# Row sums of a 64 MB array on one Trainium2 core: the wait for the last store stands on TensorE in place of SyncE

## The chip, the core and the metric

One NeuronCore of a Trainium2 chip runs the program. Its engines take part as follows: VectorE (DVE in the profile) and ScalarE (ACT) add, GpSimd (POOL) and SyncE (SP) issue transfers, and TensorE (PE) has no work. The metric is the device time of one execution in microseconds; lower is better. Each engine has a sequencer that runs its instructions in order; a wait is an instruction of its own there, and everything behind it on that engine stays back until the semaphore has the value that is asked for.

## What is computed

```python
def setup_inputs():
    batch, seq, dim = 32, 512, 1024
    return {"x": np.random.randn(batch, seq, dim).astype(np.float32)}

def reference(x: np.ndarray) -> np.ndarray:
    return np.sum(x, axis=-1).astype(np.float32)
```

16,384 rows of 1024 float32 numbers (67.1 MB) are read, and one sum for each row (65.5 KB) is written.

## The kernel before

The rows are split over the 128 partitions, so each partition has 128 rows to sum. They are loaded in blocks of 16 rows per partition (8 MB) into three buffers in turn. SyncE issues the first load alone, a half block of 8 rows per partition (L100), which a function at the end of the build (L9 to L27) moves ahead of everything else in SyncE's program. GpSimd issues all others (L102): seven whole blocks, and the last eight rows per partition in four pieces. From the third block on it waits (L156) until VectorE has summed the block whose buffer is filled again.

VectorE sums the half block and six whole blocks with one reduction each (L109). The last whole block and the last eight rows are cut small, to leave little work after the last byte: VectorE adds the halves of a row and accumulates (L118), and ScalarE copies rows into PSUM, where nobody reads them, with an accumulated sum (L138), nine rows in all. All sums stand in one tile, `sums`.

Three stores write the sums. ScalarE issues two of them after its last activation has been started (L215, L216) and then waits until both have landed (L217). SyncE issues the third: it waits for VectorE's last sum (L230) and ScalarE's last sum (L231), stores the last 16 columns of `sums` (L232, 8 KB), and waits until that store has landed (L233). That is the last instruction of the program. The build merges the wait of L230 into the store itself.

TensorE has a few instructions in all: its part in the barriers at the start of the program, recorded under L248 and L43 (the records of its sequencer carry the name PEldq), and one branch (L259) into the block that holds the kernel. In the kernel itself it has none.

After the program come instructions that are not in the kernel's file: the engines meet, the semaphores are set to zero, and the engines meet once more. The profile's span ends with the program's own last instruction, so this end lies outside of the span. It is not in any view of the page; the trace keeps the times at which semaphores were changed there.

Of the kernel before, what the change touches and what calls it, by code (L numbers as in the profile page):

```python
# [30 lines left out]
def kernel(  # L31
# [5 lines left out]
    nc = tc.nc  # L37
# [53 lines left out]
    def semaphore(name):  # L91
        return ctx.enter_context(nc.semaphore(name=name))
# [136 lines left out]
    stored = semaphore("stored")  # L229
    nc.sync.wait_ge(done, 1)  # L230
    nc.sync.wait_ge(acts, n_acts)  # L231
    nc.sync.dma_start(out=out_b[:, TWO - BIG :], in_=sums[:, J - BIG :]).then_inc(stored, 16)  # L232
    nc.sync.wait_ge(stored, 16)  # L233


# [28 lines left out]
```

## Time and profile before

| what | value |
|---|---|
| median of 3 runs | 160.44 us (160.31 to 160.48) |
| the profiled execution | 160.33 us |
| its span, first to last instruction of the program | 159.0 us |
| HBM traffic over the span | 67.11 MB read, 0.07 MB written, 422 GB/s |
| busy: VectorE, ScalarE, GpSimd | 121.6, 10.9, 6.1 us |
| the last store, issue to landing | 1.4 us |

Times in views count from the start of the span. A trailing q in an engine's name (SPq, ACTq, PEldq) means its sequencer: waits, branches and DMA issues, which do not count as busy. TensorE does not appear among the busy engines. The trace's list of semaphore changes gives a time for each change; where several engines change the same semaphore in turn, the engine is told by the order and by what it did just before.

### The profile page before, as it was taken

To read this page: it belongs to the slowest core of one execution; us is meant where nothing else is said; L and a number is where in the kernel's file an instruction comes from. 1 tells how busy PE (TensorE), PEld (TensorE's weight loads), DVE (VectorE), ACT (ScalarE), POOL (GpSimd) and SP (SyncE) were. 2 spreads that over 40 slices of the span, in tenths; PEclk is the share of its full clock that TensorE was granted. 3 is DMA by queue.
4 is the path that set the end of the run, shared out by engine and by line. 5 is a ranking of instruction groups with operands and counts; after the bars stand their busy time and mean duration, and the time that the engine had idled before them with its cause. 6 is when DMAs were issued, how large, how long until landed. Compare 5 with 4: busy or idle time off the path is not lost.

```text
span 159.0 us, 124 instructions
## 1 busy us (share of the span) xinstructions
DVE 121.6 (76%) x43; ACT 10.9 (7%) x19; POOL 6.1 (4%) x15
## 2 busy tenths in 40 slices
DVE  0000009999998999949999599986999679995986
ACT  3000000000000000000000000000000000000995
POOL 3000000010001000010000100000000220000000
DMA  7999996997969969969969979799699699698994
GB/s 264 527 396 396 396 659 264 528 462 330 527 280 511 527 264 527 527 264 527 527 264 527 478 313 527 346 445 528 264 527 527 264 528 527 264 527 349 402 407 177
DMA packets 2000, 67.18 MB, mean 422 GB/s; under 512 B 624, under 2 KB 624, under 8 KB 848
## 3 DMA queue, kind: packets, MB, share of 16 engines
q0 software_dynamic: 1424, 62.92, 91.4%
q1 hardware_dynamic: 288, 4.20, 6.6%
q10 hardware_dynamic: 288, 0.06, 0.2%
HBM read 67.11 MB, written 0.07 MB: 422 GB/s over the span
## 4 chain that ended last, share of the span: by engine, by line
DMA 73%; DVE 24%; issue 1%; POOL 0%; POOLq 0%
DMA rows<-in_x_dram 73%; DVE sums L109 22%; DVE rows L118 2%; POOL rows L102 0%; DVE ends L118 0%; DVE sums L118 0%; POOLq L43 0%
## 5 line engine op out<-in xcount | busy, mean ns | idle before, releaser
L109 DVE TENSOR_REDUCE sums<-rows 128x16 f32<-128x16384 f32 (+1 forms) x7 | 111.9, 16000 | 31.8 <-DMA rows<-in_x_dram 31.8
L138 ACT ACTIVATE unread<-rows 128x1024 f32<-128x1024 f32 x9 | 9.1, 1014 | 145.1 <-DMA rows<-in_x_dram 145.1
L118 DVE CUSTOM_DVE_ANT_0 rows<-rows 128x512 f32<-128x512 f32 (+2 forms) x15 | 8.9, 663 | 2.6 <-DMA rows<-in_x_dram 2.6
L102 POOL DMA_DIRECT2D rows<-in_x_dram x9 | 4.9, 544 | 122.0 <-DVE sums L109 120.5
L138 ACT ACTIVATION_READ_ACCUMULATOR unread<-rows 128x1 f32 x9 | 1.7, 187 | 0.0
L138 ACT ACT_TABLE_LOAD x1 | 1.3, 1283 | 1.4 <-PEq L43 1.4
L118 DVE DVE_READ_ACCUMULATOR2_ANT sums<- 128x1 f32 x15 | 1.3, 84 | 0.0
L175 DVE MEMSET ends<- 128x1 f32 x2 | 0.1, 59 | 1.5 <-PEq L43 1.5
L102 POOL DMA_DIRECT2D ends<-in_x_dram x2 | 1.1, 541 | 0.0
L118 DVE CUSTOM_DVE_ANT_0 ends<-ends 128x257 f32<-128x257 f32 (+1 forms) x2 | 0.6, 360 | 0.0
L118 DVE DVE_READ_ACCUMULATOR2_ANT ends<- 128x1 f32 x2 | 0.2, 84 | 0.0
L248 POOL MEMSET const-float32-0.0<- 128x1 f32 x1 | 0.1, 98 | 0.2 <-issue 0.2
L248 POOL MEMSET const-bfloat16-1.0<- 128x1 bf16 x1 | 0.1, 101 | 0.0
L248 POOL MEMSET const-float32-1.0<- 128x1 f32 x1 | 0.1, 98 | 0.0
L248 POOL MEMSET const-uint8-127<- 128x1 uint8 x1 | 0.1, 98 | 0.0
## 6 DMA issues: line engine op xcount, KB each, us to landing
rows<-in_x_dram SPq DMA_DIRECT2D x1, 4096.0 KB, 24.1
rows<-in_x_dram POOLq DMA_DIRECT2D x1, 2816.0 KB, 27.8
rows<-in_x_dram POOLq DMA_DIRECT2D x1, 896.0 KB, 29.5
ends<-in_x_dram POOLq DMA_DIRECT2D x1, 256.0 KB, 29.6
ends<-in_x_dram POOLq DMA_DIRECT2D x1, 128.0 KB, 29.3
rows<-in_x_dram POOLq DMA_DIRECT2D x7, 40.4
out_dram<-sums ACTq DMA_DIRECT2D x1, 48.0 KB, 1.6
out_dram<-sums ACTq DMA_DIRECT2D x1, 8.0 KB, 1.5
```

The costliest lines, as they stand in the source:

```text
L102: nc.gpsimd.dma_start(out=dst, in_=src, single_packet=True).then_inc(sem, 16)
L109: return nc.vector.tensor_reduce(out=sums[:, j : j + n], in_=block, axis=mybir.AxisListType.X, op=mybir.AluOpType.add,)
L118: return nc.vector.tensor_tensor_reduce(out=src[:, :n], in0=src[:, :n], in1=src[:, n:], scale=1.0, scalar=0.0, op0=mybir.AluOpType.add, op ...
L138: nc.scalar.activation(out=unread[n_acts % len(unread)][:, :], in_=src, func=mybir.ActivationFunctionType.Copy, accum_out=sums[:, j : j + ...
L175: nc.vector.memset(w[:, -1:], 0.0)
L248: nc = _bacc.Bacc("TRN2", target_bir_lowering=False, num_devices=1)
```

## The change

```diff
     nc.sync.wait_ge(done, 1)
     nc.sync.wait_ge(acts, n_acts)
     nc.sync.dma_start(out=out_b[:, TWO - BIG :], in_=sums[:, J - BIG :]).then_inc(stored, 16)
-    nc.sync.wait_ge(stored, 16)
+    nc.tensor.wait_ge(stored, 16)
```

The wait for the last store is taken from SyncE and given to TensorE. SyncE's program then ends with the issue of the store. On TensorE the wait comes right behind the branch into the kernel's block, so its sequencer arrives there at the start and stays until the store has landed. All other instructions and their order on each engine are unchanged.

## The prediction

> **What bounds the kernel now.** I first read the page's chain of work that ended last.
>
> ```profile
> DMA 73%; DVE 24%; issue 1%; POOL 0%; POOLq 0%
> DMA rows<-in_x_dram 73%; DVE sums L109 22%; DVE rows L118 2%; POOL rows L102 0%; DVE ends L118 0%; DVE sums L118 0%; POOLq L43 0%
> ```
>
> The loads and VectorE's sums behind them fill it. The change touches none of them: TensorE issues no load and holds no buffer. So the span up to the last store is taken as it is, and the question is what follows. The timeline's last lines (start, length, instruction) and SyncE's waits come next.
>
> ```profile
> 157.47 0.09 DVE L118 DVE_READ_ACCUMULATOR2_ANT sums<- 128x1 f32 x1
> 157.59 0.35 SPq L232 DMA_DIRECT2D out_dram<-sums  x1
> ```
>
> ```profile
> SPq L231 <- ACT unread L138: 156.1, 1, 156.1
> SPq L233 <- DMA out_dram<-sums: 1.1, 1, 1.1
> ```
>
> VectorE's last sum releases the store at 157.59 us; SyncE then sits 1.1 us in the wait that is to be moved. The views of the single waits L233 and L217 (ScalarE's, for the two earlier stores) give their places:
>
> ```profile
> L233 SPq EVENT_SEMAPHORE  x1: 17/17/17, 159.0 to 159.0; - x1
> ```
>
> ```profile
> L217 ACTq EVENT_SEMAPHORE  x1: 17/17/17, 158.3 to 158.3; - x1
> ```
>
> L233 is the last instruction; the span ends 17 ns after its start. But the execution took 160.33 us and the span 159.0, so 1.3 us lie around it, and that is where this change works. There I read the trace's list of semaphore changes. To the nanosecond, the last of the 16 steps of the store's semaphore is at 158.995 and L233 is recorded from 159.012. Of semaphore 2, which the program does not name, the list has:
>
> ```
>   1.644
> 158.431  158.469  158.513
> 159.153  159.197  159.235  159.269  159.318
> (runs of other semaphores, each changed once: 159.278 to 159.880)
> 160.104  160.138  160.177  160.221  160.244  160.343  160.381  160.415  160.462
> ```
>
> I read these as two rounds of nine, each passed along the five engines and back, with a stretch of resets between. In the first round, one engine hands on at 1.644, and only TensorE has nothing to do from then on. The next step comes at 158.431, 131 ns after ScalarE's L217; two more follow by 38 and 44 ns; then all wait for SyncE, which hands on at 159.153, 141 ns after L233. The way back takes 44, 38, 34 and 49 ns, to TensorE at 159.318. So TensorE is first in the row and SyncE last, and the late engine of today is the one with only the way back ahead of it: 159.318 - 159.153 = 165 ns. The Trainium skill bears this reading out: its page "Runtime: NRT & Kernel Launch", under "Semaphores 0–2 are reserved", calls number 2 the sync barrier.
>
> What follows hangs on TensorE too. The longest run of resets, semaphores 7 to 53, begins at 159.533, 215 ns after that last step, and ends at 159.880, when the other four runs are over by 159.681. The second round starts 224 ns later. So whatever delays 159.318 delays the end by as much.
>
> **The change, part by part.** *Taken away:* SyncE's wait. SyncE can hand on about 1.1 us earlier (its store's issue ends at 157.59 + 0.35 = 157.94 us), but it still has to be reached through TensorE, so this gains nothing by itself. Nothing stands behind L233 on SyncE and no DMA is moved; no queue is passed.
>
> *Added:* a wait on TensorE, which stands there from 1.4 us on. Queued behind it is no instruction of the program, only the hand-on that today comes at 1.644; for that, all four other engines wait in the first round. What it costs is worked out in three terms.
>
> First, how soon TensorE sees the semaphore. The barriers at the start release all engines; their records carry L43 (and L248).
>
> ```profile
> L43 SPq EVENT_SEMAPHORE  x2: 17/17/17, 1.0 to 1.3; - x2
> L43 ACTq EVENT_SEMAPHORE  x2: 17/17/17, 1.0 to 1.4; - x2
> L43 PEldq EVENT_SEMAPHORE  x2: 51/51/51, 1.0 to 1.4; - x2
> ```
>
> TensorE's such instruction takes 51 ns where SyncE's takes 17, and in these records it begins 12 ns after SyncE's (1.359 against 1.347, 1.031 against 1.019). I take 12 ns, with 0 as the lower bound since part of it may be the order of the release.
>
> Second, from that wait to the hand-on. SyncE's row is 141 ns. TensorE's only row is 1.359 to 1.644 = 285 ns. It has the branch of L259 in it, which the changed end has not. On ScalarE the same wait and branch lead to the next start in 77 ns (1.351 to 1.428), and without a branch, ahead of a drain, in 92 (0.696 to 0.788): the branch shows no price there. TensorE is slow without a branch as well: 150 ns from wait to drain (0.704 to 0.854). I therefore take 285 ns, as the one row of the engine and step in question, so 285 - 141 = +144 ns. The lower bound is ScalarE's row of 131 ns at the end, which would give -10; scaling that row by TensorE's slowness, 131 x 150 / 92 = 214, gives +73. By the Trainium skill, page "Advanced Engine Details and Errata", section "Control Flow Timing", an unconditional branch takes about 51 ns; taking that off as an estimate leaves 234 ns, and the sum below would be +0.30 us.
>
> Third, the way that is left. With TensorE late, the first engine is late, and the round goes out and back after it. The last round shows a whole one with nobody late: 160.104 to 160.462 = 358 ns (34, 39, 44, 23 out, then 99, 38, 34, 47 back). The round just ahead of the program takes 373 (-0.375 to -0.002). In place of 165 that is +193 ns, or +208 by the longer one.
>
> The sum: 12 + 144 + 193 = +349 ns, with the bounds 0 - 10 + 193 = +183 below and 12 + 144 + 208 = +364 above. Long parking of TensorE needs no further term: ahead of the program it handed on at -7.531, sat until the way back of that round, and made its step 50 ns behind its neighbour, as the 49 and 47 above. The two calm rounds and the resets stay as long as they are.
>
> The profiled execution at 160.33 us would thus become 160.68. It lies 0.11 under the median of the runs; on the median of 160.44 the forecast is **160.79 us**, 0.22% slower. Its span should grow only by 12 + (51 - 17) = 46 ns, to 159.1, as the rest lies behind it.
>
> **The rivals.** *TensorE's hand-on is cheaper than its one row.* For it speaks the branch in that row, and the scaled 214 ns; against it, that no TensorE row shows the cheaper price. The sum with 214 is 12 + 73 + 193 = +278 ns, with ScalarE's own price +183: 160.62 to 160.72. From 256 ns downward the sum stays under 0.32 us, which is 0.2%.
>
> *A round costs the same whoever is late.* Then only the first two terms count, 12 + 144 = +156 ns: 160.60. The 358 ns of the last round speak for a fixed price, the 165 ns behind SyncE's step speak against it. The Trainium skill gives the rule in "Runtime: NRT & Kernel Launch", section "The ~15µs preamble/postamble breakdown": about 355 ns for eight hops between the five engines. Its length agrees with the 358 measured; that it is paid whole after the last arrival does not agree with the 165.
>
> *The wait holds nothing back: faster.* If the step at 1.644 is not TensorE's, or TensorE takes its part in the round without having passed the wait, nobody waits for the store any more. SyncE would then answer 23 ns after the step at 158.513 (as in the last round), at 158.536 in place of 159.153: 0.617 us less, so 159.82, and faster as soon as over 0.32 us of it remain. For it: the result lands anyway before the end at 160.46. Against it: an engine runs in order, and SyncE and ScalarE both handed on only after their waits.
>
> *A dearer wake.* TensorE might need longer after 157 us in a wait than after 1; the 5 us at the launch showed no such price. If its own 285 ns came twice, the sum is 349 + 285 = +634 ns: 161.07.
>
> **How the numbers follow.** A measurement of this kernel can tell about 0.2%, 0.32 us, from no change. I give the forecast, with TensorE's price near its own row and a full round, 0.57; the cheaper hand-on 0.24; the round with a fixed price 0.06; the wait that holds nothing 0.07; the dearer wake 0.06. Slower is the forecast and the dearer wake, 0.63; same is the cheaper hand-on and the fixed round, 0.30; faster 0.07. The range has the bounds of the sum, 160.62 to 160.80, and the fixed round at 160.60; runs of the same kernel spread from 0.13 under to 0.04 over their median, so about 0.1 us is added below and 0.13 above: 160.50 to 160.93. The faster rival and the dearer wake stay outside.
>
> **What would show it.** In the profile after, L233 must be a record of TensorE's sequencer, 51 ns long, beginning about 30 ns after the store's last step, and the span about 159.1. The early step of semaphore 2 must be gone; its first step after the store must come about 0.3 us behind the last landing, and nine steps must follow one another within some 0.36 us, with no gap for SyncE. If the first step comes 0.2 us behind the landing, the second term was too large; if fewer than nine steps follow it, the order of the engines is not the one I read. A step of the round ahead of the landing, or a time under 160.1, would prove the forecast wrong altogether; so would a store that is issued or lands later, since I hold everything before it unchanged.

## The result, and the profile after

| | before | after |
|---|---|---|
| median of 22 runs each | 160.31 us (160.23 to 160.66) | 160.68 us (160.55 to 161.37) |
| ratio, 95% interval | | 1.0023, 1.0017 to 1.0029 |
| the profiled execution | 160.33 us | 160.59 us |
| its span | 159.0 us | 159.0 us |

The change makes the kernel slower by 0.23%, some 0.37 us. The span is 159.0 us in both profiled executions, so the loss is to be looked for behind it. First the page of the changed kernel: the opening, the busy engines, and the chain that ended last.

```profile
span 159.0 us, 124 instructions
DVE 121.6 (77%) x43; ACT 10.9 (7%) x19; POOL 6.2 (4%) x15
DMA 74%; DVE 22%; POOL 1%; issue 1%; POOLq 0%
```

The busy times are those of before to 0.1 us, and the transfers have 74% of the chain where they had 73% (it ends through another of the last loads, so VectorE has 22% in place of 24%). That is the same kernel up to the last store. The timeline's last lines, the view of line 233, and SyncE's waits show the end of the program:

```profile
157.37 0.08 DVE L118 DVE_READ_ACCUMULATOR2_ANT sums<- 128x1 f32 x1
157.48 0.35 SPq L232 DMA_DIRECT2D out_dram<-sums  x1
```

```profile
L233 PEldq EVENT_SEMAPHORE  x1: 51/51/51, 158.9 to 158.9; - x1
```

```profile
SPq L231 <- ACT unread L138: 156.0, 1, 156.0
SPq L43 <- PEq L43: 0.5, 2, 0.3
SPq L248 <- PEq L248: 0.2, 1, 0.2
```

The record of L233 has gone to TensorE's sequencer and takes 51 ns in place of 17, and SyncE's wait of 1.1 us for the store is no longer listed. The store is issued 0.11 us earlier than in the execution shown of before, which is where the two executions differ inside the span.

The rest is in the trace's list of semaphore changes. Here are the steps of semaphore 2 in nanoseconds from the last landing of the last store (158.995 us before, 158.894 us after), with the early step of the calm start where there is one:

```
before  early at 1.644 us; ScalarE, GpSimd, VectorE by -564, -526, -482
        158  202  240  274  323
        1109 1143 1182 1226 1249 1348 1386 1420 1467
after   no early step
        319  353  391  435  459  556  596  630  677
        1465 1500 1538 1581 1605 1703 1741 1775 1822
```

The early step is gone: it was TensorE's. All nine steps of the first round now come behind the landing, and they take 677 - 319 = 358 ns, as the calm last round does (358 ns before, 357 after). From the last step of the first round to the last of the second it is 1144 ns before and 1145 after. So the end grew by 1822 - 1467 = 355 ns. In the profiled executions the store landed 101 ns earlier after the change, and 355 - 101 = 254 ns is the 0.26 us between their times. In all eleven profiled executions of this document, the measured time is 0.12 to 0.14 us less than the time of that last step counted from the span's start: the measured time moves with the last step of semaphore 2.

### The profile page after: what moved, and what is told of

Read it like the earlier page. It is cut to its first block, busy times and chain, and to the rows that moved or that the text cites. A ratio compares the mean times of both kernels' runs of the same rounds, so it can differ in the third digit from the quotient of the medians.

```text
span 159.0 us, 124 instructions
## 1 busy us (share of the span) xinstructions
DVE 121.6 (77%) x43; ACT 10.9 (7%) x19; POOL 6.2 (4%) x15
## 4 chain that ended last, share of the span: by engine, by line
DMA 74%; DVE 22%; POOL 1%; issue 1%; POOLq 0%
DMA rows<-in_x_dram 56%; DVE sums L109 22%; DMA ends<-in_x_dram 19%; POOL rows L102 1%; DVE ends L118 0%; DVE sums L118 0%; POOLq L43 0%
```

## The experiments

All but one are edits of the kernel before, at L233; the one that doubles TensorE's wait is an edit of the changed kernel. Each is judged by two numbers: the nanoseconds from the last landing of the last store to the last step of semaphore 2 in its profile, "the tail" from here on (1467 before, 1822 after), and the ratio of its time to that of the kernel before.

**Whose place costs what.** The wait was given to each of the other three engines.

```diff
-    nc.sync.wait_ge(stored, 16)
+    nc.scalar.wait_ge(stored, 16)
```

> Position theory (a late engine pays its own step and all of the round that is left behind it): ScalarE is second in the row, 34 ns behind TensorE, so 358 - 34 = 324 ns of the round are left after its step. Landing of the store to its wait 21 ns, wait to step 131 ns (L217's row), 324 ns, then the 1.145 us to the last step: 1.62 us from the last landing to the last step of semaphore 2, against 1.467 before and 1.822 with TensorE; the time about 0.15 us over before. Rival (TensorE costs more only because its sequencer is slow): ScalarE's own step is no slower than SyncE's, so 1.47 us and no change.

```diff
-    nc.sync.wait_ge(stored, 16)
+    nc.vector.wait_ge(stored, 16)
```

> Position theory: VectorE is read as fourth in the row, 117 ns behind TensorE, so 358 - 117 = 241 ns are left after its step. Its own step is estimated from its waits at the start, 131 x 111 / 92 = 158 ns, after 28 ns to the wait: 28 + 158 + 241 + 1145 = 1.57 us from landing to the last step, about 0.10 us over before. If VectorE is third and GpSimd fourth, 285 ns are left and it is 1.62 us. Rival (own slowness alone): 1.467 + 0.011 + 0.017 = 1.50 us.

```diff
-    nc.sync.wait_ge(stored, 16)
+    nc.gpsimd.wait_ge(stored, 16)
```

> Position theory: GpSimd is read as third, 73 ns behind TensorE, so 285 ns are left after its step. Its own step has no row at the end; between ScalarE's 131 and TensorE's 290 ns it gives 1.58 to 1.74 us from landing to the last step, 0.11 to 0.27 us over before. Rival (own slowness alone): 1.46 to 1.62 us. The place that the steps show is the main thing asked for: two steps (TensorE, ScalarE) must stand before the gap, and the late one is the third.

The views of line 233 in the three kernels, ScalarE first, then VectorE, then GpSimd:

```profile
L233 ACTq EVENT_SEMAPHORE  x1: 38/38/38, 159.0 to 159.0; - x1
```

```profile
L233 DVEq EVENT_SEMAPHORE  x1: 21/21/21, 158.9 to 158.9; - x1
```

```profile
L233 POOLq EVENT_SEMAPHORE  x1: 17/17/17, 159.0 to 159.0; - x1
```

ScalarE's record is longer than its 17 of before, because the build put the waits of L217 and of the last store into one instruction; behind the single wait of L217 in the kernel before, ScalarE's step came after 131 ns. What the semaphore changes show, with the begin of the wait's record, the engine's step, and the round's last step all counted from the landing:

| engine that waits | its wait | its step | own price (step less wait) | round's end | way left | tail | ratio to before, 95% |
|---|---|---|---|---|---|---|---|
| SyncE (before) | 17 | 158 | 141 | 323 | 165 | 1467 | |
| TensorE (after) | 29 | 319 | 290 | 677 | 358 | 1822 | 1.0023 (1.0017 to 1.0029) |
| ScalarE | 21 | 173 | 152 | 496 | 323 | 1641 | 1.0015 (1.0006 to 1.0024) |
| GpSimd | 24 | 573 | 549 | 859 | 286 | 2004 | 1.0032 (1.0019 to 1.0044) |
| VectorE | 27 | 195 | 168 | 437 | 242 | 1584 | 1.0015 (1.0006 to 1.0024) |

The way left falls from 358 through 323, 286 and 242 to 165 in the order TensorE, ScalarE, GpSimd, VectorE, SyncE. With VectorE late, two steps besides TensorE's early one stand ahead of the gap; with GpSimd late one, with ScalarE none. This settles the row that had been read from one trace. ScalarE separates the theories best: its own price is only 11 ns over SyncE's, yet its tail is 174 ns longer, and 323 - 165 = 158 of those are the way left. Slowness alone asked for no change on ScalarE. VectorE's tail came to 1584 where 1570 were expected; its ratio says that it is slower than before, but is too coarse to tell it from ScalarE. GpSimd's place was the expected one, but its own price missed the bounds, and its tail with it: 549 ns, where 131 to 290 had been given.

**Is it the wait that SyncE lost?** SyncE keeps its wait, and TensorE has one as well.

```diff
+    nc.tensor.wait_ge(stored, 16)
     nc.sync.wait_ge(stored, 16)
```

> TensorE and SyncE both wait for the store. Position theory: SyncE's wait ends 17 ns after the landing and its turn comes only some 460 ns later, so it is covered: 1.82 us from landing to the last step, as with TensorE alone, and a time 0.35 us over before. Rival (the loss comes from taking the wait off SyncE, which then reaches its end in another state): 1.47 us and no change from before.

```profile
L233 PEldq EVENT_SEMAPHORE  x1: 51/51/51, 159.0 to 159.0; - x1
```

```profile
L234 SPq EVENT_SEMAPHORE  x1: 17/17/17, 158.9 to 158.9; - x1
```

These are the views of the two waits in that kernel. The record of SyncE's begins 16 ns behind the landing, its turn in the round came at 459 ns, as after the change; the tail is 1823 ns and the ratio 1.0022 (1.0012 to 1.0031). SyncE's wait is fully covered once TensorE's is there, and taking it away gained nothing.

**Is any wait on TensorE dear?** TensorE waits for ScalarE's two stores, which land earlier, and SyncE for the last one.

```diff
+    nc.tensor.wait_ge(early, 32)
     nc.sync.wait_ge(stored, 16)
```

> SyncE waits for the last store as before; TensorE waits for the two stores of ScalarE, which landed at 158.28 us in the profile before. Position theory: TensorE's step comes about 29 + 290 = 320 ns after that landing, near 158.60, and ScalarE, GpSimd and VectorE follow by 158.72, still ahead of SyncE's step at 159.15: 1.467 us from the last landing to the last step, no change. Rival (any long wait on TensorE is dear, by a wake of its sequencer or by its late hand-on): about 0.35 us over before.

```profile
L233 PEldq EVENT_SEMAPHORE  x1: 51/51/51, 158.5 to 158.5; - x1
```

```profile
L234 SPq EVENT_SEMAPHORE  x1: 17/17/17, 159.1 to 159.1; - x1
```

Again the two waits, TensorE's first. ScalarE's stores landed at 158.441 us; TensorE's wait is 660 ns ahead of the last landing and its step 370 ns ahead: 290 ns, the same price, but now under the store's flight. ScalarE, GpSimd and VectorE follow by -254, SyncE's step comes at 157, and the tail is 1465 ns with a ratio of 0.9997 (0.9987 to 1.0008). The same wait of 157 us and the same slow hand-on cost nothing where TensorE is not the last to arrive.

**What the 290 ns are made of.** First the wait was written twice.

```diff
     nc.tensor.wait_ge(stored, 16)
+    nc.tensor.wait_ge(stored, 16)
```

> The changed kernel with the wait for the store written twice on TensorE. If TensorE's 290 ns from wait to step are its ordinary price for each instruction at the end, the second wait adds one more instruction's worth, 50 to 150 ns (51 ns is the record's length, 150 the time from such a wait to the next instruction in the start's rows): 1.87 to 1.97 us from landing to the last step, 0.40 to 0.50 us over before. Rival (the 290 ns are a wake after the long wait, paid once): 1.82 to 1.85 us.

This told nothing about the price: the build put both waits into one instruction, so the program had nothing more to do than the changed kernel. Its tail of 1817 ns and its ratio of 1.0020 (1.0007 to 1.0032) repeat that kernel. Then waits for semaphores that already had their value were set around the wait for the store; the build makes of the three one wait for the store and one further instruction behind it, which holds the other two waits. This was done on TensorE, as the edit shows, and in the same way on GpSimd and on SyncE.

```diff
-    nc.sync.wait_ge(stored, 16)
+    nc.tensor.wait_ge(early, 32)
+    nc.tensor.wait_ge(stored, 16)
+    nc.tensor.wait_ge(done, 1)
```

> TensorE waits for the store and then has one more instruction, a wait for semaphores that have long had their value. Theory: the 290 ns from TensorE's wait to its step are made of ordinary instructions of a slow sequencer, so one more adds 50 to 150 ns (the record's 51, or the 150 from such a wait to the next instruction at the start): 1.87 to 1.97 us from the last landing to the last step of semaphore 2. Rival (a wake that is paid once, the rest is cheap as on SyncE, 17 to 40 ns): 1.84 to 1.86 us.

> The same on GpSimd, whose 549 ns from wait to step were above the bounds given for it. Theory: the 549 hold a fixed piece of GpSimd's end and its plain instructions are cheap (in the start's rows two such waits stand 78 ns apart, 1.227 to 1.305 us), so one more adds 20 to 80 ns to 2.004 us: 2.02 to 2.08 us. Rival: each GpSimd instruction is dear, 150 ns and more: 2.15 us or more.

> The same on SyncE, in the kernel before. One more instruction costs 20 to 70 ns there (17 is the record's length, 71 the time from such a wait to the next instruction at the start): 1.49 to 1.54 us from landing to the last step, against 1.467. Rival (the end is bound by something other than SyncE's step): 1.467 us.

The views of the two records on TensorE, on GpSimd and on SyncE:

```profile
L234 PEldq EVENT_SEMAPHORE  x1: 51/51/51, 158.9 to 158.9; - x1
```

```profile
L235 PEldq EVENT_SEMAPHORE  x1: 51/51/51, 159.0 to 159.0; - x1
```

```profile
L234 POOLq EVENT_SEMAPHORE  x1: 17/17/17, 158.9 to 158.9; - x1
```

```profile
L235 POOLq EVENT_SEMAPHORE  x1: 43/43/43, 159.0 to 159.0; - x1
```

```profile
L234 SPq EVENT_SEMAPHORE  x1: 17/17/17, 158.9 to 158.9; - x1
```

```profile
L235 SPq EVENT_SEMAPHORE  x1: 28/28/28, 159.0 to 159.0; - x1
```

| one more instruction on | step after the landing, without and with it | begin of its record, and from there to the step | tail, without and with it | ratio to before, 95% |
|---|---|---|---|---|
| TensorE | 319, 424 | 139, 285 | 1822, 1924 | 1.0023 (1.0014 to 1.0032) |
| GpSimd | 573, 659 | 90, 569 | 2004, 2091 | 1.0036 (1.0024 to 1.0049) |
| SyncE | 158, 223 | 75, 148 | 1467, 1530 | 1.0006 (0.9995 to 1.0017) |

One trivial instruction moves the step by 105 ns on TensorE, 86 on GpSimd and 65 on SyncE. The further instruction had nothing left to wait for, and yet from its record to the step it takes as long as from the single wait for the store: 285 ns against 290 on TensorE, 148 against 141 on SyncE, 569 against 549 on GpSimd (on the last two its record is 11 and 26 ns longer than the single wait's). So these prices are not those of a wake. TensorE's 290 ns are the worth of 290 / 105 = 2.8 such instructions, SyncE's 141 of 2.2; that would fit a few ordinary steps of a slower sequencer, but no trace shows what stands between the last wait and the step. GpSimd's 549 are 6.4 of them, so something else is likely to be in them; what it is stays open. GpSimd's tail went 11 ns over the range expected. The trace resolves these steps; the times of the last kernels, with intervals of about 0.2% and more in width, do not.

No placement beat the kernel before: SyncE has the shortest way left, and of the five prices in the table the lowest hand-on (ScalarE's 131 ns behind a single wait is 10 ns less, against 158 ns more of the way). A kernel with no wait for the last store was not tried, since its end would race with the store.

## Why the prediction was right

*The stage.* The span was said to grow by 46 ns only, and the cost to lie behind it. The span stayed at 159.0 us in the profiled execution, whose store came 0.11 us earlier; from the landing to the end of the record of L233, 17 + 17 = 34 ns became 29 + 51 = 80, which is the 46.

*The three terms.* They were 12, 144 and 193 ns and measured 29 - 17 = 12, 290 - 141 = 149, and 358 - 165 = 193. The sum of 349 measured 354, and 355 with a nanosecond in the resets. In time, 0.35 us on 160.44 was forecast, and 160.68 - 160.31 = 0.37 us came. The predicted 160.79 is 0.11 over the measured median because the three runs shown of before lay 0.13 over the later median of 22.

*The choice that mattered* was TensorE's price: its own start row of 285 ns, or something cheaper. The row held, at 290 ns without a branch. That the two agree to 5 ns does not show the branch to be free, as the prediction argued from ScalarE: the end may have something in its place that costs as much, and no run separates the two, so the closeness may be luck. The Trainium skill's figure of about 51 ns for a branch ("Advanced Engine Details and Errata", "Control Flow Timing") would have led to 234 ns and +0.30 us, and the measured step decides against taking it off here.

*The rivals.* The cheaper hand-on fell with those 290 ns. A round of fixed price fell with the way left, which changes with the engine from 358 to 165 ns; the about 355 ns that the Trainium skill gives for the round ahead of a program ("Runtime: NRT & Kernel Launch", "The ~15µs preamble/postamble breakdown") agree with the way left when TensorE is the late one, 358 here, and not with the 165 to 323 of the others. The wait that holds nothing fell with the early step that is gone and the first step 319 ns behind the landing. The dearer wake, which asked for TensorE's 285 ns twice, fell with the 290, and with the 285 behind a wait that held nothing. That taking SyncE's wait away gains nothing, which the prediction only argued, the kernel with both waits shows.

## What to carry to other kernels

What the end of this program costs is set by which engine arrives last: the price is that engine's own hand-on plus the part of the engines' round that is left behind it. In a kernel that ends like this one, leave the last wait to the engine at the far end of the round, if its hand-on is quick (SyncE here, 141 + 165 ns), and keep instructions off TensorE and GpSimd that become ready after the others are done. Elsewhere on the same engine a wait is free as long as something later covers it: what looks like the same edit cost 355 ns behind the last landing and nothing 0.69 us ahead of it.

## What was not expected of the hardware

GpSimd takes 549 ns from a satisfied wait to its step in the end's round, against 141 on SyncE, 131 to 152 on ScalarE, 168 on VectorE and 290 on TensorE; with this it was the dearest place of all, though it stands in the middle of the row. And the end is steady to a few nanoseconds: the stretch from the last step of the first round to that of the second was 1141 to 1147 ns in all eleven profiles.
